# Retention heads projected 512 columns at a time, and a rearranged start and end, in a two-layer fp32 decoder kernel

## The chip, the cores and the metric

The kernel runs on one core of a Trainium2 chip. The core has five engines, each with its own queue of instructions: TensorE (PE) for matmuls, VectorE (DVE) and GpSimd (POOL) for elementwise work, ScalarE (ACT) for functions, copies and casts, and SyncE (SP), which issues most DMA transfers. They wait for each other by semaphores. An engine works through its queue in order, so an instruction that waits holds up everything behind it. Matmuls write into PSUM banks (2 KB per partition, here 128 x 512 fp32), the other engines read and write SBUF and PSUM, and POOL only SBUF. The metric is device time in microseconds (us), lower is better.

## The reference

A trunk of two layers on 1024 tokens of width 1024, all in float32. Each layer is

```
mod = silu(c) @ w_ada + b_ada;  shift, scale, gate = split(mod)
h = rmsnorm(x, norm_g) * (1 + scale) + shift
proj = h @ w_in                     # one projection for all branches
y = concat(hgrn2, retention, ssd, gla)   # four branches of width 512
x = x + gate * (y @ w_out)
```

and after both layers a last RMS norm with the gain `final_g`. Retention, the branch that the change touches, has four heads of 128 columns:

```
q = rotary(q);  k = rotary(k) * dk**-0.5
o = decayed linear attention of (q, k, v), a fixed decay per head
y_b = group_rmsnorm(o, g, 4) * silu(g_in)
```

`rotary` splits a head's 128 columns into two halves of 64 (x1 and x2) and gives x1 cos − x2 sin and x1 sin + x2 cos, so it takes four products, one difference and one sum.

## The kernel before, in words

Every float32 matrix product is made of three matmuls: both factors are split into a rounded part and a rest, and hi x hi, lo x hi and hi x lo are added in PSUM. The normalised input stays in SBUF for a whole layer, transposed and split (`hh`, `hl`, one pair for each half of 512 tokens, eight chunks k of 128 input features). Weights come by DMA into a raw tile of 128 x 512 (two buffers), are cast by ACT to `whi` (line 384) and subtracted by DVE into `wlo` (line 385).

Three shapes of projection exist. The F shape (lines 399 to 401) makes transposed outputs with 512 tokens as the moving columns. The T shape (`proj_t`, lines 446 to 449) makes outputs by token: a 128-token block is the stationary operand and 256 weight columns move; all eight token blocks of a chunk k are done before the next, into four PSUM tiles that hold two blocks each, and every weight is loaded once. The output projection (line 1101) moves 512 columns of `w_out`.

The work is written as generators. A branch's own arithmetic (a "mix") is run step by step, and at each of its `yield`s the function `run` fills PE with so many nanoseconds of projection or output work from the queue `ready`. `drain(p)` then issues what is left of the generator `p`. PE's order is therefore fixed by the program text; for the start of the kernel the order of the other engines is too, and after that a list scheduler of the framework orders them.

A retention head has two T units: `ret_qk` (q and k, with the rotation at lines 823 to 828) and `vg_proj` for `rvg` (v is copied out of PSUM by DVE at line 717, g goes through SiLU on ACT at line 718). Both are queued ahead of the mix of the head before; `drain` waits for the second. `ret_mix` of the head itself then begins with 16 transposes of q and k (line 839): q of tokens 0 to 511, k of the same, and both of tokens 512 to 1023. Its first `yield` comes behind them, so nothing is filled in between them.

At the start, the conditioning vectors of layer 0 are summed by DVE (lines 294 and 296) from `w_ada`, the input is normalised two tiles at a time (`over_rms`, line 365), and the function `before(n)` inserts sums and weight splits between the first F steps. At the end, `final_after` is called after each half tile of the last residual addition; it makes the last norm's sums of squares (line 1138) and its scaling (line 1142, and for the last two tiles lines 1155 and 1179 to 1183).

Of the kernel before, what the change touches and what calls it, by code (L numbers as in the profile page):

```python
# [11 lines left out]
F32 = mybir.dt.float32  # L12
# [8 lines left out]
P = 128  # L21
# [143 lines left out]
def hybrid_trunk(ctx, nc, tc, t_in, out, gamma_c):  # L165
# [30 lines left out]
    def ps_mix(tag, bufs=1):  # L196
        return pm.tile([P, 512], F32, tag=tag, bufs=bufs, name=nm(tag))
# [60 lines left out]
    for i in range(2):  # L258
        gp.memset(ATs[i], 0.0)

    mhalf = cst.tile([P, 32], F32, name="mhalf")
    gp.memset(mhalf, -0.5)

    def rsqrt_of(ss, n, scale, eps):
# [30 lines left out]
        else:  # L295
            vec.scalar_tensor_tensor(acc, w, c_act[:, k : k + 1], acc, MUL, ADD)  # L296

    def columns_of(acc):

        n = acc.shape[1] // P  # L300
        ps = ps_mix("sc", 2)
        for j in range(n):
            pe.matmul(ps[:, j : j + 1], acc[:, j * P : (j + 1) * P], ones[:, 0:1], start=True, stop=True)
        return ps[:, 0:n]
# [60 lines left out]
                eng.tensor_scalar(out_[i], xs[:, m, :], r[:, i : i + 1], 0.0, MUL, ADD)  # L365
        return out_

    def modulated(l, half, xr):

        for k in range(KT):  # L370
            v, src = mid_t(), ps_mix("sc", 2)
            for j in range(4):
                pe.transpose(src[:, j * P : (j + 1) * P], xr[4 * half + j][:, k * P : (k + 1) * P], ident)
            act.activation(v, src, AF.Identity, bias=sh[l][:, k : k + 1], scale=gs[l][:, k : k + 1])
            hi = hh[half][:, k, :]
            act.copy(hi, v)  # L376
            vec.tensor_tensor(hl[half][:, k, :], v, hi.bitcast(F32), SUB)  # L377
            yield
# [53 lines left out]
    def proj_t(l, name, evac):  # L432

        src = t_in["wt"][l, T_UNITS[name]]
        pss = [ps_proj() for _ in range(4)]
        for s in range(4):
            raw = raw_t(512)
            nc.sync.dma_start(raw, src[:, s * 512 : (s + 1) * 512])
            hi, lo = split(raw, 512)
            for k in (2 * s, 2 * s + 1):  # L440
                j = (k % 2) * 256
                for m in range(NT):
                    o = pss[m // 2][:, (m % 2) * 256 : (m % 2) * 256 + 256]
                    hhi = hh[m // 4][:, k, (m % 4) * P : (m % 4) * P + P]
                    hlo = hl[m // 4][:, k, (m % 4) * P : (m % 4) * P + P]
                    pe.matmul(o, hhi, hi[:, j : j + 256], start=(k == 0 and m % 2 == 0), stop=False,  # L446
                              skip_group_check=True)
                    pe.matmul(o, hhi, lo[:, j : j + 256], start=False, stop=False, skip_group_check=True)  # L448
                    pe.matmul(o, hlo, hi[:, j : j + 256], start=False, stop=(k == KT - 1), skip_group_check=True)  # L449
                    if k == KT - 1 and m % 2:  # L450
                        evac(m // 2, pss[m // 2].rearrange("p (m c) -> p m c", m=2))
                    yield 320

    def proj_t_wide(l, name, evac, extra):

# [348 lines left out]
        nc.sync.dma_start(rt, t_in["rot"])  # L804
        return (rt[:, 0:512].rearrange("p (m d) -> p m d", m=NT), rt[:, 512:1024].rearrange("p (m d) -> p m d", m=NT))

    def ret_qk(l, h, tables, u):
        if not tables:
            tables.extend(ret_tables())
        cos, sin = tables  # L810

        def ev(j, ps):
            if j == 0:
                u["q"], u["k"] = vg_tiles()
            ms_ = slice(2 * j, 2 * j + 2)
            c2 = cos[:, ms_, :]
            s2 = sin[:, ms_, :]
            for qk, o in (("q", 0), ("k", 128)):
                act.copy(u[qk][:, ms_, :], ps[:, :, o : o + 128])
            for qk in ("q", "k"):  # L820
                x1, x2 = u[qk][:, ms_, 0:64], u[qk][:, ms_, 64:128]
                t = mid_t().rearrange("p (i m d) -> p i m d", i=4, m=2)
                vec.tensor_tensor(t[:, 0], x1, c2, MUL)
                vec.tensor_tensor(t[:, 1], x2, s2, MUL)
                vec.tensor_tensor(t[:, 2], x1, s2, MUL)
                vec.tensor_tensor(t[:, 3], x2, c2, MUL)
                gp.tensor_tensor(u[qk][:, ms_, 0:64], t[:, 0], t[:, 1], SUB)
                gp.tensor_tensor(u[qk][:, ms_, 64:128], t[:, 2], t[:, 3], ADD)

        yield from proj_t(l, ("rqk", h), ev)  # L830

    def ret_mix(l, h, u, between=None):
        AT = ATs[h % 2]
# [314 lines left out]
        gp.tensor_tensor(r, r, mhalf[:, 0:1], ALU.pow)  # L1148
        return r

    def final_gained(m, s):

        if m not in fin:
            fin[m] = big_t()
        vec.tensor_tensor(fin[m][:, s], xs[:, m, s], final_gain()[:, s], MUL)
        return fin[m]

    def final_after(m, nh):

        s = slice(nh * 512, nh * 512 + 512)  # L1160
        if m < NT - 1:
            if nh == 0 and m:
                final_scale(m - 1, fin["r"])
            if nh:
                ss = sm_t("ss", 1, w=8)
                scaled_squares(xs[:, m, :], ss)
                fin["r"] = final_rms(ss, EPS)
                if m == NT - 2:
                    final_gained(m, slice(0, D))
            return  # L1170
        ss = sm_t("ss", 1, w=8)
        scaled_squares(xs[:, m, s], ss)
        y = final_gained(m, s)
# [4 lines left out]
        y6 = fin[m - 1]  # L1178
        vec.tensor_scalar(y6, y6, fin["r"], None, MUL)
        nc.sync.dma_start(out[(m - 1) * P : m * P, :], y6)  # L1180
# [14 lines left out]
    def ada_load(i, k):  # L1195

        w = yp.tile([P, 512], F32, tag=("yh", "yl")[k % 2], name=nm("wa"))
        nc.sync.dma_start(w.rearrange("p (j c) -> p j c", j=2),
                          t_in["w_ada"][0, k * P : (k + 1) * P, 0 : 2 * D]
                          .rearrange("p (j c) -> p j c", j=2)[:, :, i * 256 : i * 256 + 256])  # L1200
        return w

    def ada_set(i, ps):
# [27 lines left out]
    w0 = {}  # L1231
    for m in (0, 2):
        xr += over_rms((m, m + 1), squares((m, m + 1)), (vec,))
    for i, raw in enumerate(raws):
        w0[(i, 0)] = split(raw[:, 0:512], 512)
    for k in range(KT):
        ada_step(acc[0], ada0[k], k)
    ada_set(0, columns_of(acc[0]))
    ada = ada_steps()
    wide = hgrn_vg_wide(0, 0, u, dls[0])  # L1240
    mods = [modulated(0, half, xr) for half in range(2)]

    def sums(n):
        for _ in range(n):
            next(ada, None)

    def before(n):
        if n == 1:
            for m in (4, 6):
                xr.extend(over_rms((m, m + 1), squares((m, m + 1)), (vec,)))  # L1250
            sums(KT)
            w_load(1)
        elif n in (3, 6, 10):
            ada_set(n // 3, columns_of(acc[n // 3]))
        if 3 <= n < 9:
            sums(3)
# [7 lines left out]
    first_f(0, units, order, mods, w0, pss, before, ahead=lambda n: (2, 2, 4, 5)[n] if n < 4 else n + 3)  # L1264
    start.__exit__(None, None, None)

    def load_masks():
# [14 lines left out]
    for l in range(DEPTH):  # L1282
# [66 lines left out]
        for g in range(2):  # L1349
            if g == 0:  # L1350
                px = [add(ssd_xz(l, g, u))]
            drain(px.pop())
            nu = {}
            if g == 0:
                add_out(l, (14, 15))
                p = add(ssd_bc(l, 1, nu))
            else:
                add_out(l, (8, 9))
                tables = []
                add(ret_qk(l, 0, tables, nu))  # L1360
                p = add(vg_proj(l, ("rvg", 0), nu))
# [102 lines left out]
```

## Time and profile before

| | us |
|---|---|
| three runs | 2128.68, 2127.0, 2127.72 (median 2127.72) |
| the profiled execution | 2126.23 |
| its span (first to last instruction) | 2124.3 |
| mean granted TensorE clock in it | 0.996 |

All durations below come from the profiled execution. A row of the timeline gives the start, the duration, the engine, the line of the program, the operation with output and inputs, and in brackets the idle time before it with what ended it. A group row gives the busy time, the mean of one in ns, and the idle time ahead of the group with what ended it. A row of the table by windows gives, for each engine, its busy time and its instructions, then the granted clock of TensorE as a share of full speed, the busy share of the DMA engines and their rate. In the chain of waits, `x36` counts instructions of one piece. PEld is PE's loading of stationary operands, which overlaps its matmuls.

### The profile page before, as it was taken

What the parts mean: (1) busy time and instruction counts of PE and PEld (TensorE: products, weight loads), DVE (VectorE), ACT (ScalarE), POOL (GpSimd) and SP (SyncE); (2) the same over time, 40 slices, a digit from 0 to 9 for tenths busy, and PEclk for the clock granted to TensorE, in tenths of its full rate; (3) what the DMA queues carried; (4) which work ended last, traced back from release to release, by engine and by line L of the source; (5) the groups of instructions that cost most, each with busy time, mean ns of one, the idle gap of its engine ahead of it and who ended that gap; (6) DMA issues with size and microseconds to landing.
All of it is one profiled execution on the core that took longest, in us unless ns stands there. A gap on an engine that the chain in (4) does not pass through costs nothing.

```text
span 2124.3 us, 42796 instructions
## 1 busy us (share of the span) xinstructions
PE 2059.0 (97%) x18052; PEld 1844.8 (87%) x18052; DVE 1189.1 (56%) x2390; ACT 716.1 (34%) x1604; POOL 435.1 (20%) x617
## 2 busy tenths in 40 slices
PE   4999999999999999999999999999999999999997
PEld 3797889799888899999879888888988889999996
DVE  5656743836537566544556555365564665744456
ACT  4533223432343422222273223243234242222223
POOL 1000001011125254212320010000101525501232
PEclk9999999999999999999999999999999999999999
DMA  8233221111111111111122201111111111111112
GB/s 273 71 102 104 87 89 34 34 35 37 40 42 34 41 49 32 36 41 41 35 62 69 78 31 41 41 31 37 40 40 36 35 41 45 36 41 41 41 35 100
DMA packets 67536, 115.70 MB, mean 54 GB/s; under 512 B 9584, under 2 KB 19984, under 8 KB 67344
## 3 DMA queue, kind: packets, MB, share of 16 engines
q1 hardware_dynamic: 67056, 112.24, 17.3%
q8 instruction: 142, 2.33, 0.5%
q10 hardware_dynamic: 288, 0.73, 0.1%
q14 instruction: 50, 0.41, 0.1%
HBM read 108.75 MB, written 4.19 MB: 53 GB/s over the span
## 4 chain that ended last, share of the span: by engine, by line
PE 78%; DVE 10%; ACT 5%; DMA 4%; issue 2%; POOL 1%; SPq 0%; POOLq 0%; DVEq 0%; ACTq 0%
PE pp L1101 14%; PE pp L446 11%; PE pp L449 10%; PE pp L448 10%; PE pp L399 6%; PE pp L401 5%; PE pp L400 5%; DMA wa<-in_w_ada 3%; PE ms L646 2%; DVE b L296 1%; PE sc L563 1%; PE sc L503 1%; DVE b L591 1%; DVE wlo L385 1%; PE sc L650 1%
## 5 line engine op out<-in xcount | busy, mean ns | idle before, releaser
L446 PE MATMUL pp<-whi,hh 128*128 128x256 f32 x2176 | 630.4, 290 | 0.7 <-ACT b L930 0.7
L449 PE MATMUL pp<-whi,hl 128*128 128x256 f32 x2176 | 614.3, 282 | 0.0
L448 PE MATMUL pp<-wlo,hh 128*128 128x256 f32 x2176 | 612.5, 281 | 0.0
L446 PEld LDWEIGHTS pp<-whi,hh 128*128 128x128 f32 x2176 | 410.9, 189 | 4.4 <-ACT b L930 1.6
L448 PEld LDWEIGHTS pp<-wlo,hh 128*128 128x128 f32 x2176 | 411.1, 189 | 0.8
L449 PEld LDWEIGHTS pp<-whi,hl 128*128 128x128 f32 x2176 | 408.1, 188 | 0.0
L384 ACT CAST whi<-raw 128x512 fp32r<-128x512 f32 x274 | 170.0, 622 | 588.5 <-PE pp L449 292.7
L385 DVE TENSOR_TENSOR wlo<-raw,whi 128x512 fp32r<-128x512 f32 x274 | 204.4, 749 | 267.3 <-ACT whi L384 253.9
L399 PE MATMUL pp<-hh,whi 128*128 128x512 f32 x624 | 266.1, 426 | 3.9 <-ACT hh L376 2.7
L401 PE MATMUL pp<-hl,whi 128*128 128x512 f32 x624 | 249.4, 400 | 4.1 <-DVE hl L377 4.1
L400 PE MATMUL pp<-hh,wlo 128*128 128x512 f32 x624 | 247.7, 397 | 0.0
L1106 DVE TENSOR_TENSOR xs<-xs,pp 128x512 f32<-128x512 f32 x256 | 173.2, 684 | 65.3 <-PE pp L1101 63.3
L1101 PE MATMUL pp<-whi,yh 128*128 128x512 f32 x448 | 189.3, 423 | 1.1 <-ACT b L718 1.1
L1090 POOL TENSOR_TENSOR raw<-raw,gate_b 128x512 f32<-128x512 f32 x64 | 82.7, 1295 | 509.1 <-DMA raw<-in_w_out 332.4
L1101 PE MATMUL pp<-whi,yl 128*128 128x512 f32 x448 | 175.8, 392 | 0.0
L1101 PE MATMUL pp<-wlo,yh 128*128 128x512 f32 x448 | 175.1, 391 | 0.0
L267 POOL TENSOR_SCALAR rt<-ss 128x4 f32<-128x4 f32 (+1 forms) x48 | 12.1, 252 | 708.9 <-ACT junk L520 640.3
L401 PEld LDWEIGHTS pp<-hl,whi 128*128 128x128 f32 x624 | 117.8, 189 | 35.4 <-DVE hl L377 7.6
L399 PEld LDWEIGHTS pp<-hh,whi 128*128 128x128 f32 x624 | 118.2, 189 | 28.1 <-ACT hh L376 4.3
L400 PEld LDWEIGHTS pp<-hh,wlo 128*128 128x128 f32 x624 | 118.7, 190 | 20.3 <-DVE wlo L385 0.4
L1101 PEld LDWEIGHTS pp<-whi,yh 128*128 128x128 f32 x448 | 84.4, 188 | 22.1 <-issue 3.0
L296 DVE SCALAR_TENSOR_TENSOR b<-wa,c_act,b 128x512 f32<-128x512 f32 x84 | 64.2, 764 | 69.3 <-DMA wa<-in_w_ada 68.2
(251 smaller groups left out, 3191.4 us busy)
## 6 DMA issues: line engine op xcount, KB each, us to landing
raw<-in_wt SPq DMA_DIRECT2D x136, 256.0 KB, 3.0
wa<-in_w_ada SPq DMA_DIRECT2D x96, 256.0 KB, 2.8
raw<-in_wf SPq DMA_DIRECT2D x74, 256.0 KB, 2.6
raw<-in_w_out SPq DMA_DIRECT2D x64, 256.0 KB, 2.6
xs<-in_x SPq DMA_DIRECT2D x8, 512.0 KB, 7.0
out<-b SPq DMA_DIRECT2D x7, 512.0 KB, 2.6
b<-in_wf SPq DMA_DIRECT2D x6, 256.0 KB, 6.9
b<-in_wt SPq DMA_DIRECT2D x4, 384.0 KB, 4.6
```

The source lines that it names most:

```text
L296: vec.scalar_tensor_tensor(acc, w, c_act[:, k : k + 1], acc, MUL, ADD)
L384: act.copy(hi, raw)
L385: eng.tensor_tensor(lo, raw, hi.bitcast(F32), SUB)
L399: pe.matmul(ps, hi[:, j : j + P], hh[half][:, k, :], start=(k == 0), stop=False)
L400: pe.matmul(ps, lo[:, j : j + P], hh[half][:, k, :], start=False, stop=False)
L401: pe.matmul(ps, hi[:, j : j + P], hl[half][:, k, :], start=False, stop=(k == KT - 1))
L446: pe.matmul(o, hhi, hi[:, j : j + 256], start=(k == 0 and m % 2 == 0), stop=False, skip_group_check=True)
L448: pe.matmul(o, hhi, lo[:, j : j + 256], start=False, stop=False, skip_group_check=True)
L449: pe.matmul(o, hlo, hi[:, j : j + 256], start=False, stop=(k == KT - 1), skip_group_check=True)
L1090: gp.tensor_tensor(raw, raw, gate_b[:, nh * 512 : (nh + 1) * 512], MUL)
L1101: pe.matmul(ps, a[:, o : o + P], b, start=(n == 0), stop=(n == 3 * len(kts) - 1))
L1106: vec.tensor_tensor(xv, xv, ps, ADD)
```

## The change

It has four parts.

1. Retention is projected by a new generator `ret_proj` through `proj_pair`. A raw tile now holds 256 columns of q and k and 256 of v and g for one chunk k, brought by two DMAs of 128 KB, and 512 columns move. Only four 128-token blocks are done at a time, each in a PSUM tile of its own, so the eight chunks are gone through twice, once for each half of the tokens, and every weight is loaded, cast and subtracted twice. With chunk 7 each token block is evacuated: q and k copied by ACT, v by DVE, g through SiLU by ACT, then the rotation of that one block, so that its operations are 64 columns wide where they were 2 x 64. `ret_proj` takes the place of the two units in the queue.
2. At the start the conditioning sums come ahead of the weight splits, `w_ada` of the first sums is packed on the host so that each row is one run of 2 KB, the transposes of the first two chunks are issued ahead, and the sums of later groups are spread over the F steps.
3. The constant tile `mhalf` has 8 columns in place of 32, which moves the tiles allocated after it by 96 bytes per partition, the weight buffers among them.
4. At the end, `final_scale` of a tile comes behind the squares of the next one, and `final_gained` is gone.

```diff
-    mhalf = cst.tile([P, 32], F32, name="mhalf")
+    mhalf = cst.tile([P, 8], F32, name="mhalf")
...
+    def proj_pair(l, names, evac):
+
+        src = t_in["wt"][l]
+        for half in range(2):
+            pss = [ps_proj() for _ in range(4)]
+            for k in range(KT):
+                raw = raw_t(512)
+                for i, name in enumerate(names):
+                    nc.sync.dma_start(raw[:, i * 256 : i * 256 + 256],
+                                      src[T_UNITS[name]][:, k * 256 : k * 256 + 256])
+                hi, lo = split(raw, 512)
+                for m in range(4):
+                    hhi = hh[half][:, k, m * P : m * P + P]
+                    hlo = hl[half][:, k, m * P : m * P + P]
+                    pe.matmul(pss[m], hhi, hi, start=(k == 0), stop=False)
+                    pe.matmul(pss[m], hhi, lo, start=False, stop=False)
+                    pe.matmul(pss[m], hlo, hi, start=False, stop=(k == KT - 1))
+                    if k == KT - 1:
+                        evac(4 * half + m, pss[m])
+                    yield 690
...
-    def ret_qk(l, h, tables, u):
+    def ret_proj(l, h, tables, u):
...
-        def ev(j, ps):
-            if j == 0:
+        def ev(m, ps):
+            if m == 0:
                 u["q"], u["k"] = vg_tiles()
...
+                u["v"], u["g"] = vg_tiles()
+            c2, s2 = cos[:, m, :], sin[:, m, :]
             for qk, o in (("q", 0), ("k", 128)):
-                act.copy(u[qk][:, ms_, :], ps[:, :, o : o + 128])
+                act.copy(u[qk][:, m, :], ps[:, o : o + 128])
+            vec.tensor_copy(u["v"][:, m, :], ps[:, 256:384])
+            act.activation(u["g"][:, m, :], ps[:, 384:512], AF.Silu)
             for qk in ("q", "k"):
-                x1, x2 = u[qk][:, ms_, 0:64], u[qk][:, ms_, 64:128]
-                t = mid_t().rearrange("p (i m d) -> p i m d", i=4, m=2)
+                x1, x2 = u[qk][:, m, 0:64], u[qk][:, m, 64:128]
+                t = mid_t(256).rearrange("p (i d) -> p i d", i=4)
                 vec.tensor_tensor(t[:, 0], x1, c2, MUL)
                 vec.tensor_tensor(t[:, 1], x2, s2, MUL)
                 vec.tensor_tensor(t[:, 2], x1, s2, MUL)
                 vec.tensor_tensor(t[:, 3], x2, c2, MUL)
-                gp.tensor_tensor(u[qk][:, ms_, 0:64], t[:, 0], t[:, 1], SUB)
-                gp.tensor_tensor(u[qk][:, ms_, 64:128], t[:, 2], t[:, 3], ADD)
-
-        yield from proj_t(l, ("rqk", h), ev)
+                gp.tensor_tensor(u[qk][:, m, 0:64], t[:, 0], t[:, 1], SUB)
+                gp.tensor_tensor(u[qk][:, m, 64:128], t[:, 2], t[:, 3], ADD)
+
+        yield from proj_pair(l, (("rqk", h), ("rvg", h)), ev)
...
-            if nh == 0 and m:
-                final_scale(m - 1, fin["r"])
             if nh:
                 ss = sm_t("ss", 1, w=8)
                 scaled_squares(xs[:, m, :], ss)
+                if m:
+                    final_scale(m - 1, fin["r"])
                 fin["r"] = final_rms(ss, EPS)
-                if m == NT - 2:
-                    final_gained(m, slice(0, D))
...
-    for i, raw in enumerate(raws):
-        w0[(i, 0)] = split(raw[:, 0:512], 512)
+    mods = [modulated(0, half, xr, ahead=2 * (half == 0)) for half in range(2)]
+    next(mods[0])
     for k in range(KT):
         ada_step(acc[0], ada0[k], k)
-    ada_set(0, columns_of(acc[0]))
+    w0[(0, 0)] = split(raws[0][:, 0:512], 512)
+    ada_set(0, columns_of(acc[0], ps_mix("ms")))
+    for i in (1, 2):
+        w0[(i, 0)] = split(raws[i][:, 0:512], 512)
...
     def before(n):
-        if n == 1:
-            for m in (4, 6):
-                xr.extend(over_rms((m, m + 1), squares((m, m + 1)), (vec,)))
-            sums(KT)
+        sums((0, 3, 2, 3, 3, 3, 2, 2, 2, 2, 2)[n] if n < 11 else 0)
...
-            add(ret_qk(l, h + 1, tables, nu))
-            p = add(vg_proj(l, ("rvg", h + 1), nu))
+            p = add(ret_proj(l, h + 1, tables, nu))
             run(ret_mix(l, h, u))
             drain(p)
```

Where the instructions stand is shown for two engines. First PE before the change, where a head's v and g unit ends and its own mix begins (`pp` are the PSUM tiles of a projection, `b` in the L839 rows is the tile of q or of k):

```order
L448 MATMUL pp_9593<-wlo_9759,hh_90 128x256
L449 MATMUL pp_9593<-whi_9758,hl_92 128x256
L839 MATMUL sc_9822<-cs,b_1424_9506 128x128 x4
L839 MATMUL ms_9828<-cs,b_1425_9507 128x128 x4
L839 MATMUL sc_9834<-cs,b_1424_9506 128x128 x4
L839 MATMUL po_9840<-cs,b_1425_9507 128x128 x4
L446 MATMUL pp_9847<-whi_9853,hh_89 128x256
```

The unit that ends there wrote v and g; q and k came from the unit ahead of it. The same place of PE after the change, where the second half of the tokens ends (the transposes are line 874 there, the projection lines 480 to 482):

```order
L480 MATMUL pp_9482<-whi_9620,hh_90 128x512
L481 MATMUL pp_9482<-wlo_9621,hh_90 128x512
L482 MATMUL pp_9482<-whi_9620,hl_92 128x512
L480 MATMUL pp_9483<-whi_9620,hh_90 128x512
L481 MATMUL pp_9483<-wlo_9621,hh_90 128x512
L482 MATMUL pp_9483<-whi_9620,hl_92 128x512
L874 MATMUL sc_9710<-cs,b_1468_9395 128x128 x4
L874 MATMUL ms_9716<-cs,b_1469_9396 128x128 x4
L874 MATMUL sc_9722<-cs,b_1468_9395 128x128 x4
L874 MATMUL po_9728<-cs,b_1469_9396 128x128 x4
L480 MATMUL pp_9735<-whi_9742,hh_89 128x512
```

The last projection matmuls now write the PSUM tile that holds q and k of the last 128 tokens, and the transposes of q (`b_1468`) and k (`b_1469`) are the next instructions. On DVE this is the place that belongs to it after the change, from the weights of the next head to the second of the four token blocks:

```order
L397 TENSOR_TENSOR wlo_9803<-raw_9799,whi_9802 128x512
L853 COPY b_1470_9397<-pp_9480 128x128
L858 TENSOR_TENSOR b_1508_9631<-b_1468_9395,b_1240_8314 128x64
L859 TENSOR_TENSOR b_1508_9631<-b_1468_9395,b_1240_8314 128x64
L860 TENSOR_TENSOR b_1508_9631<-b_1468_9395,b_1240_8314 128x64
L861 TENSOR_TENSOR b_1508_9631<-b_1468_9395,b_1240_8314 128x64
L858 TENSOR_TENSOR b_1509_9638<-b_1469_9396,b_1240_8314 128x64
L859 TENSOR_TENSOR b_1509_9638<-b_1469_9396,b_1240_8314 128x64
L860 TENSOR_TENSOR b_1509_9638<-b_1469_9396,b_1240_8314 128x64
L861 TENSOR_TENSOR b_1509_9638<-b_1469_9396,b_1240_8314 128x64
L853 COPY b_1470_9397<-pp_9481 128x128
L858 TENSOR_TENSOR b_1510_9652<-b_1468_9395,b_1240_8314 128x64
```

Copies of v (L853) and rotations (L858 to L861) alternate there, one copy and eight rotation operations for each token block; before, the copies of v stood in the unit behind, apart from the rotations. The end of the first half of the tokens looks the same.

More of the change, by code (lines that the diff above doesn't have):

```diff
@@ L296, in ada_step, with columns_of @@
             vec.scalar_tensor_tensor(acc, w, c_act[:, k : k + 1], acc, MUL, ADD)
-    def columns_of(acc):
+    def columns_of(acc, ps=None):
         n = acc.shape[1] // P
-        ps = ps_mix("sc", 2)
+        ps = ps_mix("sc", 2) if ps is None else ps
         for j in range(n):
@@ L366, in over_rms, with modulated, turned @@
         return out_
-    def modulated(l, half, xr):
+    def modulated(l, half, xr, ahead=0):
+        srcs = {}
+        def turned(k):
+            srcs[k] = ps_mix("sc", 2)
+            for j in range(4):
+                pe.transpose(srcs[k][:, j * P : (j + 1) * P], xr[4 * half + j][:, k * P : (k + 1) * P], ident)
+        if ahead:
+            for k in range(ahead):
+                turned(k)
+            yield
         for k in range(KT):
[L371 to L374, printed above, removed]
+            if k >= ahead:
+                turned(k)
+            v = mid_t()
+            act.activation(v, srcs[k], AF.Identity, bias=sh[l][:, k : k + 1], scale=gs[l][:, k : k + 1])
             hi = hh[half][:, k, :]
@@ L1149, in final_rms @@
         return r
[L1151 to L1156, printed above, removed]
     def final_after(m, nh):
@@ L1166, in final_after @@
                 scaled_squares(xs[:, m, :], ss)
+                if m:
+                    final_scale(m - 1, fin["r"])
                 fin["r"] = final_rms(ss, EPS)
-                if m == NT - 2:
-                    final_gained(m, slice(0, D))
             return
+        if nh == 0:
+            fin["y"] = big_t()
+        y = fin["y"]
         ss = sm_t("ss", 1, w=8)
         scaled_squares(xs[:, m, s], ss)
-        y = final_gained(m, s)
+        vec.tensor_tensor(y[:, s], xs[:, m, s], final_gain()[:, s], MUL)
         if nh == 0:
@@ L1177, in final_after @@
             return
-        y6 = fin[m - 1]
-        vec.tensor_scalar(y6, y6, fin["r"], None, MUL)
-        nc.sync.dma_start(out[(m - 1) * P : m * P, :], y6)
+        final_scale(m - 1, fin["r"])
         r = final_rms(ss, fin["t"])
@@ L1197, in ada_load @@
         w = yp.tile([P, 512], F32, tag=("yh", "yl")[k % 2], name=nm("wa"))
-        nc.sync.dma_start(w.rearrange("p (j c) -> p j c", j=2),
-                          t_in["w_ada"][0, k * P : (k + 1) * P, 0 : 2 * D]
-                          .rearrange("p (j c) -> p j c", j=2)[:, :, i * 256 : i * 256 + 256])
+        nc.sync.dma_start(w, t_in["w_ada0"][i, k])
         return w
@@ L1233, in hybrid_trunk @@
         xr += over_rms((m, m + 1), squares((m, m + 1)), (vec,))
-    for i, raw in enumerate(raws):
-        w0[(i, 0)] = split(raw[:, 0:512], 512)
+    mods = [modulated(0, half, xr, ahead=2 * (half == 0)) for half in range(2)]
+    next(mods[0])
     for k in range(KT):
         ada_step(acc[0], ada0[k], k)
-    ada_set(0, columns_of(acc[0]))
+    w0[(0, 0)] = split(raws[0][:, 0:512], 512)
+    ada_set(0, columns_of(acc[0], ps_mix("ms")))
+    for i in (1, 2):
+        w0[(i, 0)] = split(raws[i][:, 0:512], 512)
+    ss = [sm_t("ss", 2, w=8) for _ in range(2)]
+    for i in range(2):
+        sum_squares(4 + i, ss[0][:, i : i + 1])
+        next(mods[0])
+    xr += over_rms((4, 5), ss[0])
+    for i in range(2):
+        sum_squares(6 + i, ss[1][:, i : i + 1])
+    xr += over_rms((6, 7), ss[1], (vec,))
     ada = ada_steps()
     wide = hgrn_vg_wide(0, 0, u, dls[0])
-    mods = [modulated(0, half, xr) for half in range(2)]
     def sums(n):
@@ L1247, in before @@
     def before(n):
-        if n == 1:
-            for m in (4, 6):
-                xr.extend(over_rms((m, m + 1), squares((m, m + 1)), (vec,)))
-            sums(KT)
+        sums((0, 3, 2, 3, 3, 3, 2, 2, 2, 2, 2)[n] if n < 11 else 0)
+        if n in (3, 6, 10):
+            ada_set(n // 3, columns_of(acc[n // 3]))
+        if n == 3:
             w_load(1)
[L1253 to L1256, printed above, removed]
         if 5 <= n < 8:
@@ L1263, in hybrid_trunk @@
     pss = [[ps_proj(), ps_proj()], [ps_proj(), ps_proj()], [ps_mix("ms"), ps_mix("po")]]
-    first_f(0, units, order, mods, w0, pss, before, ahead=lambda n: (2, 2, 4, 5)[n] if n < 4 else n + 3)
+    first_f(0, units, order, mods, w0, pss, before, made=2,
+            ahead=lambda n: (2, 2, 4, 5)[n] if n < 4 else n + 3)
     start.__exit__(None, None, None)
@@ L1359, in hybrid_trunk @@
                 tables = []
-                add(ret_qk(l, 0, tables, nu))
-                p = add(vg_proj(l, ("rvg", 0), nu))
+                p = add(ret_proj(l, 0, tables, nu))
             run(ssd_mix(l, g, u, st, lambda: more_x(nu) if g == 0 else None))
@@ L1446 @@
         "w_ada": np.ascontiguousarray(a["w_ada"]),
+        "w_ada0": np.ascontiguousarray(a["w_ada"][0, :, : 2 * D].reshape(KT, P, 2, KT // 2, 256)
+                                       .transpose(3, 0, 1, 2, 4)).reshape(KT // 2, KT, P, 512),
         "w_out": np.ascontiguousarray(a["w_out"]),
```

3 lines of the change are left out of this document (removed).

## The prediction

> **What bounds the kernel now.** I began with the page: TensorE (PE) has almost no free time, and most of the chain that ended last is PE.
>
> ```profile
> span 2124.3 us, 42796 instructions
> PE 2059.0 (97%) x18052; PEld 1844.8 (87%) x18052; DVE 1189.1 (56%) x2390; ACT 716.1 (34%) x1604; POOL 435.1 (20%) x617
> PE 78%; DVE 10%; ACT 5%; DMA 4%; issue 2%; POOL 1%; SPq 0%; POOLq 0%; DVEq 0%; ACTq 0%
> ```
>
> Time therefore goes away only where PE issues less or faster, and comes back wherever PE waits. The stage that the change rewrites is the retention, so next the table by windows, for the stretch from one head's transposes to the next's:
>
> ```profile
> core 0: us, PE busy (x) PEld busy (x) DVE busy (x) ACT busy (x) POOL busy (x), PEclk, DMA share, GB/s
> 916.35:971.70 55.35, 55.35 (x470) 55.35 (x469) 24.92 (x64) 14.97 (x43) 11.58 (x20) 1.00 0.14 39
> ```
>
> PE is busy for the whole of it at clock 1.00, and DVE for under half. Why there is no wait shows in the timelines of PE and DVE (start, duration):
>
> ```profile
> 956.94 0.29 PE L446 MATMUL pp<-whi,hh 128*128 128x256 f32 x1
> ...
> 957.66 0.29 PE L446 MATMUL pp<-whi,hh 128*128 128x256 f32 x1
> ...
> 971.70 0.60 PE L839 MATMUL sc<-cs,b 128*128 128x128 f32 x4
> 972.14 0.60 PE L839 MATMUL ms<-cs,b 128*128 128x128 f32 x4
> 972.57 0.60 PE L839 MATMUL sc<-cs,b 128*128 128x128 f32 x4
> ```
>
> ```profile
> 947.50 0.29 DVE L823 TENSOR_TENSOR b<-b,b 128x128 f32<-128x128 f32 x1
> 947.70 0.55 DVE L824 TENSOR_TENSOR b<-b,b 128x128 f32<-128x128 f32 x1
> 948.17 0.54 DVE L825 TENSOR_TENSOR b<-b,b 128x128 f32<-128x128 f32 x1
> 948.64 0.28 DVE L826 TENSOR_TENSOR b<-b,b 128x128 f32<-128x128 f32 x1
> 948.84 0.28 DVE L823 TENSOR_TENSOR b<-b,b 128x128 f32<-128x128 f32 x1
> ...
> 956.92 0.28 DVE L826 TENSOR_TENSOR b<-b,b 128x128 f32<-128x128 f32 x1
> 957.13 1.55 DVE L385 TENSOR_TENSOR wlo<-raw,whi 128x512 fp32r<-128x512 f32 x2
> ```
>
> The rotation (L823 to L828) of the next head's q and k runs on DVE until 957.13, and the transposes that read it (L839) start at 971.70. In between PE works at the v and g unit. That 14.6 us distance is what the change touches.
>
> **Wider matmuls.** Three matmuls of 256 columns take (957.66 − 956.94)/2 = 0.36 us, two such triples 0.72. The nearest rows for 512 columns are the output projection in the chain (36 in a row) and the first stage's projections:
>
> ```profile
> 1891.02 8.21 PE pp L1101 x36
> ```
>
> ```profile
> 30.14 0.39 PE L399 MATMUL pp<-hh,whi 128*128 128x512 f32 x1
> ...
> 30.84 0.39 PE L399 MATMUL pp<-hh,whi 128*128 128x512 f32 x1
> ```
>
> That is 8.21/36 = 0.228, a triple 0.684; or 0.70. Eight heads have 1024 narrow triples (2 units x 8 x 8 each), now 512 wide ones: 512 x (0.72 − 0.684) = **−18 us**, bounds −10 (at 0.70) and −20 (at 0.68).
>
> **Wait A, at the end of each head.** In the changed order PE's last projection matmuls of a head are followed at once by the 16 transposes of the same head, in all eight places; nothing stands between. They read q and k of tokens 4 to 7, whose sums finished only now. The rotation of these four tiles is 32 DVE operations 64 columns wide, with a v copy ahead of each eight, and 16 on POOL. The rows near them:
>
> ```profile
> L597 DVE TENSOR_TENSOR b<-b 128x128 f32<-128x128 f32 x12 | 3.5, 289 | 0.2
> L888 DVE TENSOR_TENSOR b<-b 128x64 f32<-128x64 f32 x14 | 3.1, 224 | 0.3
> L654 DVE COPY st<-ms 128x128 f32<-128x128 f32 x24 | 7.0, 291 | 37.9 <-PE ms L646 37.9
> L827 POOL TENSOR_TENSOR b<-b 128x128 f32<-128x128 f32 x8 | 4.9, 616 | 9.7 <-DVE b L825 9.7
> L828 POOL TENSOR_TENSOR b<-b 128x128 f32<-128x128 f32 x8 | 4.4, 548 | 0.0
> ```
>
> A group of four 128-column operations takes 948.84 − 947.50 = 1.34 us: two starts are 0.2 apart and two 0.47, those that run beside POOL's L827 and L828. Half the columns save 65 ns in the unhindered operation (289 to 224), so 0.14; the hindered one is between 0.14 (no hindrance) and 0.47 (it does not shrink). A group then takes 0.56 to 1.2, with 1.34 as the outer bound if nothing shrinks; I take 0.91, the hindered operation at 0.32. The Trainium skill, "SBUF — State Buffer", section "Who interferes with whom", says that a DVE instruction with two SBUF inputs contends with a GpSimd instruction that reads SBUF; the 0.55 beside 0.28 above agrees, and without that rule the group would be 0.56.
>
> Count from the end of the first tile's last matmul. Two ACT copies and the v copy come first, so the rotation starts at about 1.0. One tile takes 2 x 0.91 + 0.29 = 2.11, so the fourth tile's q group starts at 1.0 + 3 x 2.11 = 7.3, ends at 8.2, and with POOL's last operations q is there at 8.7 and k at 9.6. PE has the other three tiles (2.06) and two sets of four transposes (972.57 − 971.70 = 0.87) to do, so it wants q at 2.93. It waits 5.8, then 0.5 for k, with signals about 6.5 us: eight times **+52**. Bounds: at a group of 0.56, q at 6.2 and 3.5 us (+28); at 1.34, 9.6 us (+77).
>
> **The clock after A.** PE at rest can come back slow:
>
> ```profile
> 2091.30 0.50 PE L1101 MATMUL pp<-wlo,y 128*128 128x512 f32 x1 [1.88 <-DVE wlo L385]
> ```
>
> ```profile
> 2091.30:2094.70 3.40, 3.40 (x9) 2.67 (x10) 1.84 (x3) 0.47 (x1) 0.00 (x0) 0.56 0.00 0
> 88.20:91.40 3.20, 3.20 (x74) 2.87 (x73) 2.58 (x8) 1.50 (x3) 0.00 (x0) 0.50 0.10 19
> 1061.60:1065.00 3.40, 3.37 (x15) 2.75 (x16) 2.38 (x4) 1.15 (x2) 0.00 (x0) 1.00 0.50 159
> ```
>
> After 1.88 us idle, 3.4 us went at 0.56 once; after an equal wait at 1061.63 the clock stayed 1.00. A stretch of 3.4 us at half speed loses 1.7 us. Once per head is 8 x 1.7 = **+14**, bounds 0 and 27 (also after wait B). The Trainium skill, "TensorE: Matmul & The Clock Gate", section "The HAM clock gate (the \"warmup\" mystery)", gives half speed after an idle window of about 3.4 us; by it alone A, at 6.5, would pay all 14 and B nothing, while the 1.88 us above shows that less can be enough.
>
> **Wait B, between the token halves.** Four PSUM tiles take the projection; the second half's four sums reuse those of the first half. Each is free when DVE has copied v out and ACT has applied the SiLU behind it:
>
> ```profile
> L718 ACT ACTIVATE b<-pp 128x256 f32<-128x256 f32 x88 | 33.3, 384 | 80.7 <-DVE b L717 80.7
> ```
>
> ACT waits there for the DVE copy already. In the new DVE order each copy stands behind eight rotation operations of the tile before. The fourth copy ends at 1.0 + 3 x 2.11 = 7.3, the SiLU at 7.7; PE wants this buffer at 2.06 + 3 x 0.69 = 4.1. So 3.5 us, spread over three short waits: **+28**, bounds 1.5 each (+12) at a group of 0.56 and 6 (+48) at 1.34.
>
> **Weights.** Loaded twice, they cost 64 more casts and 64 more subtractions, and each raw tile now comes by two DMAs of 128 KB:
>
> ```profile
> L384 ACT CAST whi<-raw 128x512 fp32r<-128x512 f32 x274 | 170.0, 622 | 588.5 <-PE pp L449 292.7
> L385 DVE TENSOR_TENSOR wlo<-raw,whi 128x512 fp32r<-128x512 f32 x274 | 204.4, 749 | 267.3 <-ACT whi L384 253.9
> raw<-in_wt SPq DMA_DIRECT2D x136, 256.0 KB, 3.0
> ```
>
> Per head DVE gains 8 x 0.75 = 6 and about 3 of fixed rotation cost over its 25 of 55, so there is room. A tile lasts PE 4 x 0.684 = 2.7 us, and the two raw buffers bring one every (3.0 + 0.62 + 0.75 + 0.3)/2 = 2.3. I take 0; if the DMAs do not overlap the cover is gone, and that is a rival below.
>
> **Start, end, offset.** At the start PE waits for DVE, which does eight conditioning sums before the subtraction (L377) that PE needs; before them stand three weight splits:
>
> ```profile
> 40.87 0.79 PE L401 MATMUL pp<-hl,whi 128*128 128x512 f32 x1 [3.86 <-DVE hl L377]
> ```
>
> ```profile
> 36.95:40.80 3.85, 0.06 (x1) 0.00 (x0) 3.71 (x7) 0.59 (x1) 0.00 (x0) 0.50 0.96 289
> ```
>
> At most 3.86, the 1.7 us of slow clock behind it, and three splits of 0.75 that now follow the sums: −7.8. The DMA share of 0.96 says that data will take some of it back, and the splits may hold the first matmul instead (+2). I take **−4**. At the end DVE loses a pass of 1024 columns (the wider of the two below) and gains another, fused one elsewhere:
>
> ```profile
> 2115.64 1.82 DVE L1155 TENSOR_TENSOR b<-xs,b 128x1024 f32<-128x1024 f32 x2
> ```
>
> Two passes in 1.82 us hold the chain's end; I take **−1** (0 to −2). The shorter constant tile shifts later buffers by 96 bytes; no row prices that, and I take 0 within ±2.
>
> **Sum**, on the profiled execution (2126.2; its span 2124.3 and 1.9 around it; the median of the runs is 1.5 higher, and I leave that out): −18 + 52 + 14 + 28 − 4 − 1 = +71, so **2197 us**. All low bounds give 2126 + 28 + 0 + 12 − 20 − 7.8 − 2 − 2 = 2134; all high ones 2126 + 77 + 27 + 48 − 10 + 2 + 2 = 2272.
>
> **Rivals.**
> - *No wait (0.13).* PE finds q and k in time, because the DVE and POOL work ends with PE's own last tile. For it: DVE is under half busy in the windows. Against: 28 rotation operations and three copies have to fit into 2.93 us, and even at 0.14 and 0.29 each they take 4.8. It decides below 2.9 us from first sum to last q. Time 2126 − 23 = 2103.
> - *One short wait (0.13).* Only A at its lower bound, with the copies of B taken early and no slow clock: 2126 − 23 + 28 = 2131. For it: the equal wait at 1061.63 kept 1.00. Against: DVE's order puts rotations between the copies. It decides where hindrance disappears.
> - *Starved weights (0.08), slower too.* If the two DMAs into a tile land one behind the other, two buffers take (6.0 + 1.7)/2 = 3.8 per tile against 2.7; 128 tiles lose up to 1.1 each, in part in the shadow of A: about 70 on top, 2197 + 70 = 2267. Against it: 39 GB/s and a DMA share of 0.14 in the windows.
> - *The matmul is no cheaper (part of the forecast's width).* At 0.72 per wide triple the term −18 is 0: 2215.
>
> **Chances and range.** The forecast with both waits has 0.66, no wait 0.13, one short wait 0.13, starvation 0.08. Its own range is 2140 to 2255. For 8 in 10 I leave out the no-wait case and the far end of starvation: 2125 to 2255. A change of under 0.2% (4 us) counts as none: no wait is faster, the short wait is split between the same (0.04), faster (0.02) and slower (0.07), which gives faster 0.15, same 0.04, slower 0.81.
>
> **What would show it.** In the changed kernel's retention, from the last projection matmul of a head to the third set of transposes, a PE wait of 3.5 to 10 us that ends on POOL or on ACT's copy of q; half a clock in the window behind it; three waits of about 1 us at the start of each second half, ending on ACT's SiLU; matmuls 0.228 apart elsewhere. PE idle would rise by about 80 us in all. The forecast is wrong if the transposes follow the projection with less than 2 us of idle time, if a DVE group of four at 64 columns takes under 0.4, or if waits end on DMA.

## The result, and the profile after

The changed kernel takes 2187.06 us (median of four runs, 2186.01 to 2189.3) against 2128.08 for the kernel before: a ratio of 1.0279, 95% interval 1.0261 to 1.0297. It is 59 us slower; 71 was forecast, and 2197 us. The profiled execution took 2188.07 us, 62 more than that of before.

The page of the changed kernel, with the lines that answer to those shown of before, and the group of the new projection's first matmul:

```profile
span 2186.3 us, 40947 instructions
PE 2065.7 (94%) x16516; PEld 1777.9 (81%) x16516; DVE 1242.0 (57%) x2739; ACT 771.1 (35%) x1768; POOL 461.6 (21%) x747
PE 74%; DVE 12%; ACT 5%; DMA 4%; issue 2%; POOL 2%; SPq 0%; POOLq 0%; DVEq 0%; ACTq 0%
...
L480 PE MATMUL pp<-whi,hh 128*128 128x512 f32 x512 | 212.8, 416 | 13.8 <-ACT b L854 13.7
```

PE's busy time hardly grew (2059 to 2066); its idle time did, from 3% to 6% of the span. The waits of PE in the changed kernel (time in all, number, longest) say for whom:

```profile
PE sc L874 <- POOL b L863: 42.2, 29, 4.2
PE pp L480 <- ACT b L854: 13.7, 12, 1.5
...
PE sc L303 <- DVE b L296: 7.0, 2, 3.5
```

The first two rows are waits A and B of the prediction. The third is at the start of the kernel, where the prediction had a gain. Here is one wait A in PE's timeline, between the second and the third head of the first layer:

```profile
929.61 0.39 PE L482 MATMUL pp<-whi,hl 128*128 128x512 f32 x1
929.84 0.60 PE L874 MATMUL sc<-cs,b 128*128 128x128 f32 x4
930.27 0.60 PE L874 MATMUL ms<-cs,b 128*128 128x128 f32 x4
931.46 0.33 PE L874 MATMUL sc<-cs,b 128*128 128x128 f32 x1 [0.58 <-POOL b L863]
933.57 0.33 PE L874 MATMUL sc<-cs,b 128*128 128x128 f32 x1 [1.79 <-POOL b L863]
934.68 0.33 PE L874 MATMUL sc<-cs,b 128*128 128x128 f32 x1 [0.79 <-POOL b L863]
936.24 0.47 PE L874 MATMUL sc<-cs,b 128*128 128x128 f32 x1 [1.23 <-POOL b L863]
936.50 1.06 PE L874 MATMUL po<-cs,b 128*128 128x128 f32 x4
937.22 0.78 PE L480 MATMUL pp<-whi,hh 128*128 128x512 f32 x1
```

The transposes of q of tokens 4 to 7 go one at a time, each when GpSimd's last operation of its rotation has ended; those of k follow with hardly a wait. The 16 transposes take 937.22 − 929.84 = 7.38 us where they took 1.67 (that is 973.37 − 971.70 in the trace of before). The eight stretches are 8.88, 7.38, 6.86, 9.80, 10.96, 6.86, 6.86 and 11.12; less 8 x 1.67, wait A is 55.4 us.

The clock behind it, in the table by windows (4 us from the end of the transposes; the ninth column, ahead of the DMA share, is the granted clock):

```profile
937.22:941.22 4.00, 4.00 (x19) 3.43 (x18) 1.23 (x2) 0.70 (x2) 0.00 (x0) 0.74 0.22 59
...
1992.54:1996.54 4.00, 4.00 (x14) 3.42 (x15) 0.75 (x1) 0.59 (x1) 0.00 (x0) 0.50 0.24 70
```

All eight windows lie between 0.50 and 0.74, with a mean of 0.66, which loses 8 x 4 x 0.34 = 11 us. The clock also fell once behind a wait B: it was 0.50 from 908.60 to 912.00, which loses another 1.7. Elsewhere the wide triple is as forecast, (981.56 − 980.20)/2 = 0.68:

```profile
980.20 0.39 PE L480 MATMUL pp<-whi,hh 128*128 128x512 f32 x1
...
981.56 0.39 PE L480 MATMUL pp<-whi,hh 128*128 128x512 f32 x1
```

And the two waits at the start, with the sums that DVE was doing:

```profile
54.32 1.02 PE L303 MATMUL sc<-cs,b 128*128 128x1 f32 x8 [3.53 <-DVE b L296]
...
71.92 1.45 PE L303 MATMUL sc<-cs,b 128*128 128x1 f32 x8 [3.48 <-DVE b L296]
```

```profile
52.64 1.53 DVE L296 SCALAR_TENSOR_TENSOR b<-wa,c_act,b 128x512 f32<-128x512 f32 x2
```

**The ledger of the 62 us.** The same PE instruction (a state matmul of the first branch) starts at 135.12 before and 142.50 after: the start costs +7.4. From there to 780.79 (785.04 after, just ahead of the first wide matmul) PE's order is the same in both, and the lag falls to 4.25: −3.1 in the first layer, taken twice −6. A is +55, the clock behind it +11 and behind B +2, B +14, the matmuls 512 x (0.72 − 0.68) = −20, the tail behind the last matmul −0.7 (10.5 to 9.8). Together that is about the whole 62.

### The profile page after: what moved, and what is told of

Its sections match the earlier page's. It is cut to its first block, busy times and chain, and to the rows that moved or that the text cites. A ratio compares the mean times of both kernels' runs of the same rounds, so it can differ in the third digit from the quotient of the medians.

```text
span 2186.3 us, 40947 instructions
## 1 busy us (share of the span) xinstructions
PE 2065.7 (94%) x16516; PEld 1777.9 (81%) x16516; DVE 1242.0 (57%) x2739; ACT 771.1 (35%) x1768; POOL 461.6 (21%) x747
## 4 chain that ended last, share of the span: by engine, by line
PE 74%; DVE 12%; ACT 5%; DMA 4%; issue 2%; POOL 2%; SPq 0%; POOLq 0%; DVEq 0%; ACTq 0%
PE pp L1136 13%; PE pp L411 6%; PE pp L413 5%; PE pp L458 5%; PE pp L412 5%; PE pp L460 5%; PE pp L461 5%; PE pp L480 5%; PE pp L482 4%; PE pp L481 4%; DMA wa<-in_w_ada 3%; PE ms L679 2%; DVE b L296 1%; PE sc L596 1%; DVE b L624 1%
## 5 line engine op out<-in xcount | busy, mean ns | idle before, releaser
L397 DVE TENSOR_TENSOR wlo<-raw,whi 128x512 fp32r<-128x512 f32 x338 | 247.1, 734 | 323.5 <-ACT whi L396 310.6
L458 PE MATMUL pp<-whi,hh 128*128 128x256 f32 x1152 | 335.8, 291 | 0.7 <-ACT b L965 0.7
L460 PE MATMUL pp<-wlo,hh 128*128 128x256 f32 x1152 | 325.7, 283 | 0.0
L461 PE MATMUL pp<-whi,hl 128*128 128x256 f32 x1152 | 325.6, 283 | 0.0
L480 PE MATMUL pp<-whi,hh 128*128 128x512 f32 x512 | 212.8, 416 | 13.8 <-ACT b L854 13.7
L458 PEld LDWEIGHTS pp<-whi,hh 128*128 128x128 f32 x1152 | 220.5, 191 | 4.0 <-ACT b L965 1.5
L460 PEld LDWEIGHTS pp<-wlo,hh 128*128 128x128 f32 x1152 | 220.7, 192 | 0.1
L461 PEld LDWEIGHTS pp<-whi,hl 128*128 128x128 f32 x1152 | 220.4, 191 | 0.0
L481 PE MATMUL pp<-wlo,hh 128*128 128x512 f32 x512 | 202.2, 395 | 0.0
L482 PE MATMUL pp<-whi,hl 128*128 128x512 f32 x512 | 202.2, 395 | 0.0
L1125 POOL TENSOR_TENSOR raw<-raw,gate_b 128x512 f32<-128x512 f32 x64 | 84.3, 1319 | 512.8 <-DMA raw<-in_w_out 414.3
```

The source lines that it names most:

```text
L397: eng.tensor_tensor(lo, raw, hi.bitcast(F32), SUB)
L480: pe.matmul(pss[m], hhi, hi, start=(k == 0), stop=False)
L481: pe.matmul(pss[m], hhi, lo, start=False, stop=False)
L482: pe.matmul(pss[m], hlo, hi, start=False, stop=(k == KT - 1))
```

## The experiments

In each comparison the kernel before ran on the same chip; its median was 2127.72, 2126.65, 2126.98 and 2128.37 in the four groups. Where runs of two groups are compared, the difference is that of their distances from their own kernel before.

**The four parts, each alone.** The kernel before, with one part of the diff at a time, of which a few lines are shown.

Retention alone:

```diff
-            add(ret_qk(l, h + 1, tables, nu))
-            p = add(vg_proj(l, ("rvg", h + 1), nu))
+            p = add(ret_proj(l, h + 1, tables, nu))
```

> The kernel before with the retention part of the change alone (wide projection, rotation one token block at a time); start, end and constant tile as before. Theory: all of the loss and more comes from here, because PE waits at each head's transposes (A) and at each second half (B): about +60 us on 2128, that is 2183 to 2192, with eight PE waits of 5 to 9 us ending on GpSimd's rotation. Rival (the loss sits in the start or in the shifted buffers): 2128 - 18 = 2110, or at most half of the +59.

Measured: 2196.04, ratio 1.0317 (1.03 to 1.0334), +68. Its waits:

```profile
PE sc L862 <- POOL b L851: 39.6, 31, 2.6
...
PE pp L468 <- ACT b L842: 12.3, 14, 1.5
```

The loss is in this part, and more of it than in the whole change. Its eight stretches of transposes sum to 66.0, so A is 52.7 here. The forecast 2183 to 2192 was too low by some us: at the old place of the weight tiles the wide triple is longer, which the part on places takes up.

Start alone:

```diff
+        sums((0, 3, 2, 3, 3, 3, 2, 2, 2, 2, 2)[n] if n < 11 else 0)
```

> The kernel before with the start part alone. Theory, from the two traces: the sums spread over the F steps come late, PE waits 3.5 us twice for them (and runs at half clock behind each wait), so about +7.5 us: 2133 to 2138. Rival (the prediction's own term): -4 us, 2124. If the first stage is 2 us earlier but the end is the same, the loss was not the sums.

Measured: 2132.69, ratio 1.0028 (1.0018 to 1.0037), +5.0, just under the range of the theory. The sums come late here too:

```profile
PE sc L303 <- DVE b L296: 6.9, 2, 3.5
```

Constant tile alone:

```diff
-    mhalf = cst.tile([P, 32], F32, name="mhalf")
+    mhalf = cst.tile([P, 8], F32, name="mhalf")
```

> The kernel before with the constant tile of 8 columns in place of 32 alone: only the addresses of later tiles move, by 96 bytes. Theory, from the drift between the two traces in stages whose instruction order is the same: the F shape's matmuls are some ns shorter, about -8 us over both layers: 2118 to 2122. Rival (the prediction's term): 0 within 2 us, 2126 to 2130; then the drift comes from something else.

Measured: 2117.6, ratio 0.9952 (0.9937 to 0.9967), −10.1, a little more than forecast. The drift between the traces is the buffers' place.

End alone:

```diff
-            if nh == 0 and m:
-                final_scale(m - 1, fin["r"])
             if nh:
                 ss = sm_t("ss", 1, w=8)
                 scaled_squares(xs[:, m, :], ss)
+                if m:
+                    final_scale(m - 1, fin["r"])
```

> The kernel before with the end part alone (final scaling behind the squares). Expected by the prediction -1 us (0 to -2), by the two tails -0.7 us: 2126 to 2128. Rival: no change or a loss, if the scaling now stands ahead of the last addition.

Measured: 2125.85, ratio 0.9988 (0.9979 to 0.9997), −1.9, with runs from 2121.17 to 2128.5, so not told apart from the −0.7 of the tails. The four parts sum to 68.3 + 5.0 − 10.1 − 1.9 = +61; the whole change is +59.

**Where the retention loses.** Three kernels with the retention part alone, each with a mend. First, the second token half's transposes are put behind filling work:

```diff
         for half in range(2):
+            if half:
+                yield 9000
             for src, dst, tag in ((u["q"], QT, "sc"), (u["k"], KTt, ("ms", "po")[half])):
```

> The retention part alone, with 9 us of filling work issued between the first and the second token half's transposes of each head; nothing else differs. Theory (wait A is the transposes' place in PE's order): A, about 55 us, and the slow clock behind it vanish; the copies behind the rotation now hold the next head's first four sums (a wait like B, about 2 us, eight times more): 2128 - 18 + 20 (B) + 16 = about 2146, range 2125 to 2155. Rival (the DVE, GpSimd or weight work itself is the limit, wherever the transposes stand): the time stays above 2170.

Measured: 2159.43, ratio 1.0145 (1.0128 to 1.0162): 36 us less than the retention part, so the transposes' place is most of it, but 4 above the range given. No wait for the rotation is left in PE's list. What came in its place is a wait that I had not named:

```profile
PE sc L671 <- DVE st L677: 17.2, 6, 4.1
...
PE pp L468 <- ACT b L842: 7.8, 12, 1.4
```

```profile
945.83 0.60 DVE L677 SCALAR_TENSOR_TENSOR st<-st,ms 128x128 f32<-128x128 f32 x2
946.36 0.28 DVE L841 COPY b<-pp 128x128 f32<-128x128 f32 x1
...
953.03 0.21 DVE L849 TENSOR_TENSOR b<-b,b 128x64 f32<-128x64 f32 x1
953.17 0.28 DVE L677 SCALAR_TENSOR_TENSOR st<-st,ms 128x128 f32<-128x128 f32 x1
```

A state update of the scan (L677), for which PE waits, stands in DVE's order behind the rotation of a whole token half of the next head, from 946.36 to 953.17. Four of the six waits are of this kind, 4.0 us each, and in the 4 us behind each of them the granted clock was 0.50; the other two, of 0.6, are in the kernel before as well. The wait B did not double either: 7.8 here, and 4.2 ahead of the output projection's matmuls.

Second, the rotation comes after the four evacuations, on pairs of blocks; the transposes stay:

```diff
+            if m % 4 == 3:
+                rotate(m - 3)
+                rotate(m - 1)
```

> The retention part alone, with the rotation of a token half emitted after its four evacuations and on pairs of blocks (128 columns, half as many instructions); the transposes stay where they were. Theory: B vanishes (about -20 us), A shrinks a little, to about 5.5 us eight times, since four 128-column groups need 1.34 us each from 2.6 us on: about 2155, range 2140 to 2170. Rival (B is not the copies but the PSUM tiles or the weights): B's waits stay and the time is above 2175.

Measured: 2176.4, ratio 1.0233 (1.0218 to 1.0248), 19 us less than the retention part, and above the range, where the rival had put it. But the rival's cause does not hold: B shrinks to two short waits, one in the first head of each layer (2.5 us in all), so it was the copies behind the rotation. A hardly shrinks: its stretches sum to 61.5, less 13.3 is 48 us (53 in the retention part).

```profile
PE sc L868 <- POOL b L857: 33.2, 12, 4.6
...
PE po L868 <- POOL b L857: 5.1, 8, 1.0
```

Third, both mends:

> The retention part alone, with both edits: rotation after the evacuations, and 9 us of filling work ahead of the second half's transposes. Theory: no wait is left and the wider matmuls' gain shows: 2128 - 18 = 2110, range 2106 to 2118. Rival (loading each weight twice, or the extra DVE work, costs PE time of its own): above 2122.

Measured: 2124.49, ratio 0.9992 (0.9983 to 1.0001): 70 us less than the retention part, and equal to the kernel before. A, the clock behind it and the wait for the state are gone, and of B the same 2.5 us are left. In a head in the middle of a layer, loading every weight twice costs PE nothing that shows: PE is busy throughout, in 54.27 us where it took 55.37:

```profile
971.46:1025.73 54.27, 54.27 (x277) 45.12 (x276) 27.60 (x70) 18.82 (x55) 16.33 (x23) 1.00 0.26 74
```

The forecast of 2110 was missed, and the time lies where the rival put it. Two reasons show. A head gains 1.1, not 2.3, because a wide triple is 0.70 at this place of the weights: 64 x (0.72 − 0.70) = 1.1 to 1.3. And in the first and the last head of a layer the filling work is the output projection, which finds new waits:

```profile
PE pp L1132 <- ACT b L841: 3.3, 4, 1.8
PE pp L1132 <- DVE y L533: 3.1, 1, 3.1
```

At two places of this filling work the clock fell too, to 0.50 (1036.05 to 1039.46 and 2060.04 to 2063.45). Whether the doubled casts and subtractions have a part in these waits, as the rival would have it, is not shown.

The same with the constant tile of 8 columns and the change's end:

> The same as the last one, with the change's constant tile of 8 columns and its end, and the start as before. Theory: the shifted buffers add their gain of about 8 and the end 0.7: 2101, range 2096 to 2112, faster than both kernels. Rival (the drift in the traces is not the buffers' place): as without it, 2110.

Measured: 2113.15, ratio 0.9931 (0.9916 to 0.9945), just above the range. This beats both kernels, 14 us under the one before, but the wide projection has at most 4 of them (the constant tile alone gave 2117.6, measured in another group, and the end has a part too). A head takes 53.48 against 55.31 with the constant tile alone; what the other waits take back is shown above.

**What sets the length of A.** The rotation's last two operations on VectorE in place of GpSimd:

```diff
-                gp.tensor_tensor(u[qk][:, m, 0:64], t[:, 0], t[:, 1], SUB)
-                gp.tensor_tensor(u[qk][:, m, 64:128], t[:, 2], t[:, 3], ADD)
+                vec.tensor_tensor(u[qk][:, m, 0:64], t[:, 0], t[:, 1], SUB)
+                vec.tensor_tensor(u[qk][:, m, 64:128], t[:, 2], t[:, 3], ADD)
```

> The retention part alone, with the rotation's difference and sum on VectorE in place of GpSimd. Theory (GpSimd and its contention set the length of wait A, not VectorE's own work): six VectorE operations of 0.14 us are 0.82 a group and hold no lock, so A falls from about 6.9 to about 5.1 us, eight times -1.8, while the copies come 0.1 to 0.7 later (B +5): 2180 to 2192. Rival (VectorE's own work sets the length): a third more of it makes A and B longer, above 2200.

Measured: 2192.47, ratio 1.0314 (1.0298 to 1.0331), 3 less than the retention part, which the runs alone do not tell apart. Its stretches sum to 61.3, so A is 48 where it was 53: six operations on one engine are a little quicker than four on it beside two on the other. The waits now end on DVE and are as many:

```profile
PE sc L862 <- DVE b L851: 37.0, 27, 2.6
...
PE pp L468 <- ACT b L842: 14.1, 18, 1.2
```

So taking GpSimd out of the rotation saves only about 5 of A's 53. That is net of the two operations more that VectorE then has, so what the contention costs by itself is not shown. Putting the transposes elsewhere takes all of A away. The time falls just outside the theory's range; its saving of 14 in A was too large.

**The start.** The start part, with the sums issued ahead of their use:

```diff
-        sums((0, 3, 2, 3, 3, 3, 2, 2, 2, 2, 2)[n] if n < 11 else 0)
+        sums((0, 3, 3, 4, 4, 4, 3, 3)[n] if n < 8 else 0)
```

> The start part alone, with the later conditioning sums issued ahead of their use (3, 3, 4, 4, 4, 3, 3 from the first step on) in place of 3, 2, 3, 3, 3, 2, 2, 2, 2, 2. Theory (the start lost because the eighth sum of a group stands in the very step that needs the group, and the loads behind it start late): the two waits of 3.5 us go and the stage ends at least 5 us earlier than with the start part: 2122 to 2129. Rival (the loss comes from the packed w_ada or from the early transposes): 2131 to 2135, as the start part.

Measured: 2125.41, ratio 0.9994 (0.9985 to 1.0004), 7 less than the start part. No PE wait for L296 at L303 of the later groups is left in its list. With the change's numbers the sums in all come to 3, 5, 8 and then 11, 14, 16: the eighth and the sixteenth stood in the very steps that use them (the third and the sixth). One more sum per step, from the second on, is enough. Against the kernel before nothing is gained that can be told.

**The place of the buffers.** In the kernel before hh and hl stand at a multiple of 64 bytes, the weight tiles 32 bytes off. First, all of them are put 32 bytes off:

```diff
+    shift = cst.tile([P, 8], F32, name="shift")
+    gp.memset(shift, 0.0)
     hh = [cst.tile([P, KT, 512], F32R, name=f"hh{i}") for i in range(2)]
...
-    mhalf = cst.tile([P, 32], F32, name="mhalf")
+    mhalf = cst.tile([P, 24], F32, name="mhalf")
```

> The kernel before with 32 bytes put ahead of the activation tiles hh and hl and 32 taken from the constant tile: hh and hl move from 0 to 32 modulo 64, the weight tiles stay at 32. Theory (the two operands of a 512-column matmul are read slower when their places differ modulo 64; the output projection, with both at 32, was fast all along): the F shape's matmuls fall from 234 to 227 ns and the time is that of the 8-column constant tile, 2114 to 2121. Rival (a weight tile that is not on a multiple of 64 is slow by itself): 2126 to 2130, and the F shape stays at 234.

Measured: 2112.63, ratio 0.9937 (0.9919 to 0.9955), −14. The time is about that of the theory (1 us under its range), but its reason is not: the F shape stayed at 234 ns a matmul, and the T shape, which the constant tile had left alone, became shorter. Then the fourth combination, hh and hl 32 off and the weights on a multiple of 64, with the change's start (sums early) and end and the narrow retention:

```diff
+    shift = cst.tile([P, 8], F32, name="shift")
+    gp.memset(shift, 0.0)
```

> The kernel before with its narrow retention units, the change's end, the start with the sums issued early, and 32 bytes ahead of hh and hl, so that hh and hl stand at 32 modulo 64 and the weight tiles at 0. Theory (each shape follows one tile's own place: the F shape the weight tile's, 229 ns a matmul at 0 and 234 at 32; the T shape the place of hh, 117.6 ns at 32 and 119.7 at 0): both gains come together, 2127 - 10 - 14 - 2 - 2 = 2099, range 2094 to 2106. Rival (what counts is whether both operands stand alike): both gains are lost, F at 234 and T at 119.7, 2120 to 2125.

Measured: 2124.39, ratio 0.9983 (0.9973 to 0.9993): both gains are lost, as the rival said. The table gives the mean length of a triple, as the sum of the mean distances from one matmul's start to the next one's (neighbours that are both of the shape and less than 0.5 us apart, over the whole trace from 130 us on):

| hh and hl mod 64 | weights mod 64 | F triple, 512 columns | T triple, 256 columns | kernel |
|---|---|---|---|---|
| 0 | 32 | 732 ns | 369 ns | before |
| 0 | 0 | 718 | 368 | constant tile of 8 columns |
| 32 | 32 | 731 | 362 | all 32 off |
| 32 | 0 | 732 | 369 | the last one |

624 F triples x 14 ns = 9 us and 2176 T triples x 7 ns = 15 us are the two measured gains. Both come only where the two operands stand alike, and then in one shape or the other. Why the shape differs stays open.

## Why the prediction was right, point by point, and where it was not

The forecast that the wait at the head ends outweighs the wider matmuls holds: the trace names it, and moving the transposes and the rotation takes 70 us back, which is the retention part's loss of 68 and some of the matmuls' gain.

- **Wider matmuls, −18.** Right, −20 by the trace of the changed kernel. At the weights' old place it would have been the lower bound of the prediction: 719 ns in the kernel with both mends, so 2 x 369 − 719 = 19 ns, 512 of them −10.
- **Wait A, +52.** 55. Its mechanism is as told, but its parts are not. The group was reckoned at 0.91. At the head end shown the groups of the first three tiles took about the 0.56 of the lower bound, and GpSimd, far behind, set the pace; at the next one (from 992.26 on) the two engines took turns, a group took 0.75 to 0.79, and it was GpSimd that waited for DVE. In four of the eight heads (the first and last of a layer) GpSimd's part also stands behind scalings of output weights (L1125, 1.3 us each), which the prediction did not count and no run tested alone; those stretches are the long ones, 8.9 to 11.1, the others 6.9 to 7.4. So four heads waited 5.3 on average and four 8.5, where each was to wait 6.5: that the sum comes so near is in part luck.
- **The clock behind A, +14.** 11, and 2 behind one of the waits B: over the 4 us behind each of the eight waits the mean clock was 0.50 to 0.74. Part of the slow time lay in the wait itself (0.50 from 935.92 on at the head end shown), where PE had little to do. The Trainium skill's page "TensorE: Matmul & The Clock Gate", section "The HAM clock gate (the \"warmup\" mystery)", asks for an idle window of about 3.4 us; here no single gap inside the transposes of 929.84 to 937.22 exceeded 1.8, and the clock fell, so shorter gaps in a row were enough.
- **Wait B, +28.** 14, near the lower bound of 12. The step that failed is the size of the group, 0.91, in the first tiles. At the half boundary in front of 971.90 the four copies start at 966.20, 967.48, 968.76 and 971.26: the first two tiles take 1.28 each, unhindered, since GpSimd was still held up behind them, so the fourth copy comes 5.06 after the first where 6.3 was reckoned. In the kernel with the rotation after the evacuations B is 2.5, so its cause was right.
- **Weights, 0.** Right: no PE wait of the retention ends on a weight tile or a DMA, and the starved-weights rival falls with the 54.27 us of a head in which PE never waits.
- **Start, −4.** Wrong sign, and outside its bounds: +5.0 alone. The prediction looked only at the wait that the change removes (3.86 became 1.57) and not at the later steps, where the sums now come in the step that needs them.
- **End, −1.** −0.7 by the traces; the runs alone leave −0.6 to −4.5.
- **Offset, 0 within ±2.** Wrong: −10 alone, and −6 by the ledger of the whole change. No row of before had two placements of one shape, so no row could price it.

The errors cancel in part. By the ledger B was 14 too large, the start 11 too low and the offset 6 too high, so that 2197 stands only 10 above 2187 is luck; the signs and the order of the two main waits are not.

## What to carry to other kernels

When a product is made later and its consumer stays where it was, look at what stands between the two in the order of the waiting engine; an engine that issues in order stalls for the whole of what stands in between, however low the mean load of the others. If a unit is merged to save matmul time, move its consumer and its evacuation with it: here the two mends were worth 70 us, the wider matmuls 10 to 20 by the traces, of which 2 to 4 were left in the time. And measure where the two operands of a matmul stand in memory: in these kernels 32 bytes were worth 10 and 14 us, more than the change of shape.

## What the runs showed of the hardware that was not expected

GpSimd's small operations can be held up far beyond their own length by VectorE. In the timeline of GpSimd (changed kernel, the head end shown above) two in a row took 1.3 us and then the same kind took 0.31:

```profile
930.09 1.32 POOL L863 TENSOR_TENSOR b<-b 128x64 f32<-128x64 f32 x1
931.37 1.32 POOL L862 TENSOR_TENSOR b<-b 128x64 f32<-128x64 f32 x1
932.64 0.31 POOL L863 TENSOR_TENSOR b<-b 128x64 f32<-128x64 f32 x1
```

```profile
931.14 0.28 DVE L853 COPY b<-pp 128x128 f32<-128x128 f32 x1
...
932.02 0.21 DVE L859 TENSOR_TENSOR b<-b,b 128x64 f32<-128x64 f32 x1
...
932.42 0.28 DVE L853 COPY b<-pp 128x128 f32<-128x128 f32 x1
932.99 0.32 DVE L858 TENSOR_TENSOR b<-b,b 128x64 f32<-128x64 f32 x1 [0.29 <-POOL b L863]
933.24 0.35 DVE L859 TENSOR_TENSOR b<-b,b 128x64 f32<-128x64 f32 x1
```

While DVE ran its operations back to back at 0.21, GpSimd's were 1.32, and each of the two ended within DVE's next copy from PSUM (931.14 to 931.42 and 932.42 to 932.70), so one got through for each tile's eight products. When DVE had to wait for GpSimd, GpSimd's fell to 0.31 and DVE's rose to 0.35. At the next head end (991.74 to 997.39) both went on alternately, GpSimd's at 0.32 to 0.36 and DVE's at 0.21 to 0.36. The Trainium skill, "SBUF — State Buffer", section "Who interferes with whom", has the two engines share a port; a share in which one of them is starved for several instructions of the other is what this trace adds. And an operand's place modulo 64 bytes is worth about 5 ns on a 512-column matmul or 2 ns on a 256-column one, by the table above.
